# One-hot rows by a float32 compare on VectorE, a fourth buffer for table pieces, and another place for block 1's gates in a decoder layer

## The chip, the cores and the metric

The kernel runs on one core of one Trainium2 chip. TensorE (PE) multiplies, VectorE (DVE) and ScalarE (ACT) do element-wise work, GpSimd (POOL) asks for indirect gathers, SyncE (SP) asks for the plain transfers; 16 DMA engines move the data. Each engine works through its own list of instructions in order and waits at semaphores for the others. The metric is the device time of one execution in microseconds, less is better. The trace is of one profiled execution.

## What is computed

One decoder layer on 256 tokens of width 1024. Two attention parts come first; the change lies in the last part, product-key retrieval of single-neuron experts. Each of 8 heads picks 16 experts for a token, so that a token has 128; an expert's number is 128 x first index + second index:

```python
def peer(x, w_query, sub_keys_1, sub_keys_2, expert_down, expert_up):
    ...
    experts = jnp.take_along_axis(cand_idx, pos, axis=-1)
    gates = jax.nn.softmax(top_s, axis=-1)
    def block(args):
        xt, et, gt = args
        u = expert_down[et]
        act = jax.nn.gelu(jnp.einsum('td,tkd->tk', xt, u).astype(jnp.float32), approximate=False)
        vv = expert_up[et]
        return jnp.einsum('tk,tkd->td', (gt * act).astype(xt.dtype), vv)
```

Both tables have 16384 rows of 1024 float32 numbers, 64 MB each.

## The kernel before

The 256 tokens are two blocks of 128. After the attention parts, the top 16 experts of each head are picked on DVE (`pick`). From there the two blocks go different ways.

**Block 0 gathers.** `down` asks on GpSimd for one row of `expert_down` per token and pick, 128 gathers of 128 rows (a gather is called a *row* here: `gd`, 512 KB, five buffers), and DVE multiplies each with the block's hidden state and sums it into a column of `wt` (L899). Every 16 columns pass the gelu and are multiplied with their gates.

**Block 1 is dense.** `dense` reads the whole `expert_down` table, transposed, in 128 *pieces* of 128 experts (`d`, 512 KB each, three buffers, asked for by SyncE at L913) and multiplies each with the block's hidden state: 8 float32 matmuls of 128x128 a piece into PSUM (`sc`). Four pieces make a group; ScalarE takes the gelu of it into `W1` (expert's second index on partitions, then first index, then token).

**Spreading the gates.** `weights(b)` turns a block's 128 gates per token into the same layout. For each token one matmul is made (`wb`) of two one-hot matrices: `oa` on DVE (L1010; first index compared with 0 to 127, times the gate; four buffers) and `o2`, the second index compared with 0 to 127. `o2` is made for 8 tokens at a time: DVE compares in bf16 with the token innermost (`eq`, L990, against the table `iot8`), and ScalarE copies it to float32 with the token outermost (L1006). ScalarE brings four tokens' results from PSUM into `W0` (L1014). `weights(1)` spreads block 1's gates; `gates()` then multiplies them into `W1` for the first 27 groups (DVE, L1021), or copies them there for the last 5 groups (ScalarE, L1023), whose gelu is multiplied on later (L926). `weights(0)` then spreads block 0's finished weights into the same `W0`, and its transpose `tr` needs all 128 columns of `wt`.

**The up products.** For each of 128 pieces of `expert_up` (`u`), ScalarE and DVE split it in two float32r parts (`uh` L1153, `ul` L1154) and PE multiplies both blocks' weights with it. For 384 of the 1024 columns of block 0, up rows are gathered instead (`gu`, L931) and summed on DVE.

**Order.** A loop over `now` = 0 to 127 takes one row per step and, paced by `pace`, some dense pieces (`DPACE`) and some tokens of `weights(1)` (`SCAT1`). At step 78 the earlier buffers are closed. After the loop come the rest of `weights(1)`, all of `gates()`, and then a loop over 128 tokens of block 0 with the remaining pieces. A scheduler then sets the order on each engine from these priorities; only the up products keep the written order.

## Time and profile before

| | |
|---|---|
| time, median of 3 runs | 1080.87 us (1079.47 to 1081.7) |
| profiled execution | 1090.83 us |
| its span | 1089.0 us |
| mean granted clock of TensorE | 0.955 |
| PE busy | 947.3 us, 87% |
| DVE busy | 812.1 us, 75% |
| ACT busy | 479.2 us, 44% |
| POOL busy | 377.1 us, 35% |

Busy time is that of instructions that compute; idle time of an engine is put down to what ended it. Times in rows are us from the start of the span. The records of a float32 128x128 matmul come in pairs, so that a piece has 16 records and a token 2.

### The profile page before, as it was taken

How to read it: one execution, taken by the hardware profiler on the slowest of the kernel's cores; microseconds unless marked ns; L12 is line 12 of the kernel's file. 1: busy time of each engine (PE TensorE's matmuls, PEld its weight loads, DVE VectorE, ACT ScalarE, POOL GpSimd, SP SyncE). 2: the span in 40 equal slices, each digit the busy share in tenths (PEclk: the TensorE clock that was granted, in tenths of full speed). 3: DMA queues.
4: the chain of work that ended last, by engine and by line, in shares of the span. 5: the costliest groups of instructions: out<-in, count | busy, mean ns of one | idle time of the engine just before them, and what ended most of it. 6: DMA issues, size and time to landing. Idle time of an engine off the chain costs nothing.

```text
span 1089.0 us, 17849 instructions
## 1 busy us (share of the span) xinstructions
PE 947.3 (87%) x6650; PEld 881.0 (81%) x6650; DVE 812.1 (75%) x1944; ACT 479.2 (44%) x712; POOL 377.1 (35%) x263
## 2 busy tenths in 40 slices
PE   7999999897647957877788899899899999999994
PEld 6999879887547957766688799898788888888883
DVE  6957867556876987885478743765588888888887
ACT  5547664452101232221234344366655555555551
POOL 0000000001445452223345400000277777777773
PEclk9999999898888988999899999999899999999998
DMA  8454325444989789898899987744399999999992
GB/s 300 157 193 162 111 80 191 157 179 145 331 287 359 262 322 337 326 325 315 326 357 397 384 314 226 217 155 135 109 331 321 321 310 327 318 324 316 322 320 101
DMA packets 73974, 285.13 MB, mean 262 GB/s; under 512 B 9488, under 2 KB 10016, under 8 KB 67872
## 3 DMA queue, kind: packets, MB, share of 16 engines
q1 hardware_dynamic: 46976, 190.66, 50.2%
q0 software_dynamic: 26624, 92.29, 23.4%
q8 instruction: 52, 0.85, 0.3%
q10 hardware_dynamic: 288, 1.05, 0.3%
q14 instruction: 34, 0.28, 0.1%
HBM read 282.91 MB, written 1.05 MB: 261 GB/s over the span
## 4 chain that ended last, share of the span: by engine, by line
PE 68%; DMA 19%; DVE 6%; ACT 4%; issue 2%; POOL 0%; SPq 0%; ACTq 0%; DVEq 0%; POOLq 0%
PE py L74 27%; PE mm L74 18%; DMA d<-dnT 16%; PE sc L74 14%; PE wb L74 4%; DMA gd<-dn,ei 2%; PE tp L78 1%; DMA w<-xo 1%; DVE gd L899 1%; PE go L74 1%; ACT whi L235 1%; DVE wlo L237 1%; PE ks L74 1%; PE xo L74 1%; ACT o L1006 1%
## 5 line engine op out<-in xcount | busy, mean ns | idle before, releaser
L74 PE MATMUL sc<-h2T,d 128*128 128x128 f32 x2048 | 263.2, 287 | 61.6 <-DMA d<-dnT 58.8
L897 POOL DMA_INDIRECT gd<-dn,ei x128 | 151.7, 1185 | 469.4 <-ACT s1b L875 267.4
L74 PEld LDWEIGHTS sc<-h2T,d 128*128 128x128 f32 x2048 | 250.7, 201 | 69.8 <-DMA d<-dnT 42.9
L931 POOL DMA_INDIRECT gu<-upg,ei x128 | 220.7, 1724 | 224.3 <-DMA d<-dnT 144.0
L74 PE MATMUL py<-uh,w 128*128 128x320 f32 (+1 forms) x1024 | 234.5, 350 | 1.0 <-ACT uh L1153 1.0
L74 PEld LDWEIGHTS py<-uh,w 128*128 128x128 f32 x1024 | 176.4, 188 | 22.6 <-ACT uh L1153 1.2
L1153 ACT ACTIVATE uh<-u 128x1024 fp32r<-128x1024 f32 x128 | 135.8, 1062 | 117.5 <-PE py L74 117.5
L1154 DVE TENSOR_TENSOR ul<-u,uh 128x1024 fp32r<-128x1024 f32 x128 | 156.4, 1223 | 31.1 <-ACT uh L1153 31.1
L899 DVE CUSTOM_DVE_ANT_0 gd<-gd,h 128x1024 f32<-128x1024 f32 x128 | 154.4, 1218 | 20.8 <-DMA gd<-dn,ei 20.6
L74 PE MATMUL py<-ul,w 128*128 128x320 f32 (+1 forms) x512 | 138.3, 350 | 0.7 <-DVE ul L1154 0.7
L237 DVE TENSOR_TENSOR wlo<-w,whi 128x1024 fp32r<-128x1024 f32 (+1 forms) x68 | 81.3, 1197 | 47.4 <-PE mm L74 35.7
L1010 DVE TENSOR_SCALAR oa<-ii,ixT,wT 128x128 f32<-128x128 f32 x256 | 72.0, 347 | 56.7 <-PE wb L74 55.6
L74 PEld LDWEIGHTS py<-ul,w 128*128 128x128 f32 x512 | 90.7, 188 | 12.5 <-DVE ul L1154 1.0
L235 ACT ACTIVATE whi<-w 128x1024 fp32r<-128x1024 f32 (+1 forms) x68 | 70.4, 1039 | 54.2 <-PE mm L74 40.3
L74 PE MATMUL wb<-oa,o 128*128 128x128 f32 x512 | 73.1, 288 | 8.5 <-ACT o L1006 7.3
L1122 DVE SCALAR_TENSOR_TENSOR yq<-gu,wt,yq 128x384 f32<-128x384 f32 x127 | 77.9, 614 | 0.2
L74 PEld LDWEIGHTS wb<-oa,o 128*128 128x128 f32 x512 | 67.1, 201 | 9.8 <-ACT o L1006 7.9
L1014 ACT ACTIVATE W<-wb 128x512 f32<-128x512 f32 x64 | 37.9, 599 | 83.8 <-PE wb L74 83.2
L922 ACT ACTIVATE W<-sc 128x512 f32<-128x512 f32 x27 | 16.1, 598 | 116.9 <-PE sc L74 116.9
L1006 ACT ACTIVATE o<-eq 128x1024 f32<-128x1024 bf16 x32 | 65.8, 2072 | 1.8 <-DVE eq L990 1.8
L74 PE MATMUL mm<-whi,xPh 128*128 128x256 f32 (+1 forms) x176 | 50.8, 291 | 6.7 <-ACT xPh L244 6.7
L74 PE MATMUL mm<-h2T,w 128*128 128x128 f32 x448 | 54.0, 281 | 2.8 <-DMA w<-pq 2.8
(329 smaller groups left out, 1438.6 us busy)
## 6 DMA issues: line engine op xcount, KB each, us to landing
d<-dnT SPq DMA_DIRECT2D x128, 512.0 KB, 5.4
u<-upd SPq DMA_DIRECT2D x128, 512.0 KB, 4.7
w<-pq SPq DMA_DIRECT2D x10, 1024.0 KB, 5.8
w<-xo SPq DMA_DIRECT2D x8, 1024.0 KB, 4.8
w<-xk SPq DMA_DIRECT2D x4, 1024.0 KB, 5.4
w<-xv SPq DMA_DIRECT2D x4, 1024.0 KB, 4.8
w<-wo SPq DMA_DIRECT2D x4, 1024.0 KB, 4.8
w<-xq SPq DMA_DIRECT2D x4, 1024.0 KB, 4.8
```

The source lines that it names most:

```text
L74: self.eng.matmul(out, lhsT=lhsT, rhs=rhs, **kw)
L235: act.activation(hi, src, AF.Copy)
L237: eng.tensor_sub(lo, src, hi.bitcast(FT))
L897: gp.indirect_dma_start(out=g, out_offset=None, in_=I["dn"], in_offset=bass.IndirectOffsetOnAxis(ap=ei[:, k:k + 1], axis=0))
L899: vec.tensor_tensor_reduce(out=g, in0=g, in1=H2[0], scale=1.0, scalar=0.0, op0=OP.mult, op1=OP.add, accum_out=wt[:, k:k + 1])
L931: gp.indirect_dma_start(out=g, out_offset=None, in_=I["upg"], in_offset=bass.IndirectOffsetOnAxis(ap=PK[b]["ei"][:, k:k + 1], axis=0))
L1006: act.activation(o2, equal(b, 4 * g).rearrange("p k t -> p t k"), AF.Copy)
L1010: vec.tensor_scalar(a, iot, ixT[:, t:t + 1], wT[:, t:t + 1], op0=OP.is_equal, op1=OP.mult)
L1014: act.activation(W[0][:, :, 4 * g - 4:4 * g], ps[g - 1].rearrange("p (j i) -> p i j", j=4), AF.Copy)
L1122: vec.scalar_tensor_tensor(y, g, wt[:, k:k + 1], y, op0=OP.mult, op1=OP.add)
L1153: act.activation(uh, u, AF.Copy)
L1154: vec.tensor_sub(ul, u, uh.bitcast(FT))
```

## The change

The one-hot of the second index is written by DVE at once, as float32 and with the token outermost; the bf16 index, the table `iot8` and ScalarE's copy go. The pieces `d` get four buffers instead of three, and in the last loop every second piece uses one of the gathers' five. `SCAT1` ends at step 104 and not 116; 20 groups and not 27 come ahead of the gates, at nearly the same pace, up to step 103; the gates are taken at steps 104 to 110 of the gather loop and not behind it; from step 109 one piece is taken a step. The late groups' gelu shares the buffers of `o2`, and the gathered up rows have buffers of their own.

```diff
-SCAT1 = (80, 116)
-DENSE = 27
-DPACE = (46, 122)
+SCAT1 = (80, 104)
+DENSE = 20
+DPACE = 46
+DLATE = 1
 AHEAD = 2
+UH = 4
...
-        PK[b]["ix2"] = keep.tile([128, 128], BF, tag="ix2", name="ix2")
+        PK[b]["ix2"] = keep.tile([128, 128], FT, tag="ix2", name="ix2")
...
-                d = ust.tile([128, 8, 128], FT, tag="uh", name="d", bufs=3)
+                pool, tag, bufs = (gath, "gd", 5) if now == 127 and m % 2 else (ust, "uh", UH)
+                d = pool.tile([128, 8, 128], FT, tag=tag, name="d", bufs=bufs)
...
-                a = sml.tile([128, 4, 128], FT, tag="eq", name="ge", bufs=4)
+                a = ul_pool.tile([128, 4, 128], FT, tag="ul", name="ge", bufs=3)
...
-        g = sml.tile([128, 2 * CG], FT, tag="eq", name="gu", bufs=4)
+        g = sml2.tile([128, 2 * CG], FT, tag="gu", name="gu", bufs=4)
...
-        wT = sml2.tile([128, 128], FT, tag="wT", name="wT", bufs=2)
+        wT = sml2.tile([128, 128], FT, tag="wT", name="wT", bufs=1)
...
-                    act.activation(o2, equal(b, 4 * g).rearrange("p k t -> p t k"), AF.Copy)
+                    vec.tensor_tensor(o2, iot[:, None, :].to_broadcast([128, 8, 128]),
+                                      ix2[:, 4 * g:4 * g + 8, None].to_broadcast([128, 8, 128]), op=OP.is_equal)
...
         if 1 in W:
-            pace("dn", gd, 4 * DENSE, DPACE)
+            pace("dn", gd, 4 * DENSE, (DPACE, SCAT1[1] - 1))
         if 0 in W:
             pace("w1", gw[1], 133, SCAT1)
-    drain(gw[1], gates())
+        if now >= SCAT1[1]:
+            pace("gates", gg, 32, (SCAT1[1], SCAT1[1] + 6))
+        if now >= SCAT1[1] + 5 and now % DLATE == 0:
+            take(gd, 1)
+            at["dn"] += 1
     rest_d = 128 - 4 * DENSE
...
-        uh = ust.tile([128, DM], FR, tag="uh", name="uh", bufs=3)
+        uh = ust.tile([128, DM], FR, tag="uh", name="uh", bufs=UH)
```

What the scheduler makes of it, at three places. In these rows `ISA gd,wt` is the product of a gathered row with the hidden state and `ISA wt` its sum; `o` is `o2`. Line numbers of the change are two higher up to L990.

DVE, in the middle of the gathers, before: one stretch between two compares.

```order
L990 TENSOR_TENSOR eq<-iot_3906,ix_4802 128x1024
L1010 TENSOR_SCALAR oa<-ii,ixT,wT 128x128 x3
L899 ISA gd,wt<-gd,h_2923 128x1024
L899 ISA wt 128x1
L899 ISA gd,wt<-gd,h_2923 128x1024
L899 ISA wt 128x1
L1010 TENSOR_SCALAR oa<-ii,ixT,wT 128x128 x4
```

The same place in the change:

```order
L1008 TENSOR_SCALAR oa<-ii,ixT,wT 128x128 x5
L901 ISA gd,wt<-gd,h_2921 128x1024
L901 ISA wt 128x1
L901 ISA gd,wt<-gd,h_2921 128x1024
L901 ISA wt 128x1
L1008 TENSOR_SCALAR oa<-ii,ixT,wT 128x128 x6
L1003 TENSOR_TENSOR o_5444<-ii,ix_4787 128x1024
```

Between two pairs of rows there now stand five or six tokens, where three or four stood.

DVE, behind the last gathered row, before (the last `ISA wt` stands right ahead of it):

```order
L1010 TENSOR_SCALAR oa<-ii,ixT,wT 128x128 x8
L990 TENSOR_TENSOR eq<-iot_3906,ix_4802 128x1024
L1010 TENSOR_SCALAR oa<-ii,ixT,wT 128x128 x7
L990 TENSOR_TENSOR eq<-iot_3906,ix_4089 128x1024
L1010 TENSOR_SCALAR oa<-ii,ixT,wT 128x128 x8
L990 TENSOR_TENSOR eq<-iot_3906,ix_4089 128x1024
L1010 TENSOR_SCALAR oa<-ii,ixT,wT 128x128 x7
L990 TENSOR_TENSOR eq<-iot_3906,ix_4089 128x1024
L1010 TENSOR_SCALAR oa<-ii,ixT,wT 128x128 x11
L990 TENSOR_TENSOR eq<-iot_3906,ix_4089 128x1024
L1010 TENSOR_SCALAR oa<-ii,ixT,wT 128x128 x9
L1021 TENSOR_TENSOR W_3905<-W_3905,W_4835 128x512 x26
```

The end of the gathers in the change:

```order
L901 ISA gd,wt<-gd,h_2921 128x1024
L901 ISA wt 128x1
L1019 TENSOR_TENSOR W_3903<-W_3903,W_4821 128x512 x20
L929 TENSOR_TENSOR W_3903<-W_3903,ge 128x512 x2
L901 ISA gd,wt<-gd,h_2921 128x1024
L901 ISA wt 128x1
L901 ISA gd,wt<-gd,h_2921 128x1024
L901 ISA wt 128x1
L901 ISA gd,wt<-gd,h_2921 128x1024
L901 ISA wt 128x1
L906 TENSOR_TENSOR wt<-wt,gt 128x16
L929 TENSOR_TENSOR W_3903<-W_3903,ge 128x512
```

Block 1's 50 tokens that stood behind the last row are gone from there, and 20 gate multiplies and two late groups stand ahead of the last three rows.

PE, around the transpose of block 0's weights (`tr`), before:

```order
L74 MATMUL sc<-h2T,d 128x128 x16
L74 MATMUL wb<-oa,o_5969 128x128 x2
L74 MATMUL sc<-h2T,d 128x128 x72
L78 MATMUL tr<-ii,wt 128x128
L74 MATMUL wb<-oa,o_6211 128x128 x5
L74 MATMUL sc<-h2T,d 128x128
L74 MATMUL wb<-oa,o_6211 128x128 x2
L74 MATMUL sc<-h2T,d 128x128 x7
L74 MATMUL wb<-oa,o_6211 128x128
L74 MATMUL wb<-oa,o_6253 128x128 x5
L74 MATMUL sc<-h2T,d 128x128 x8
```

The same place in the change:

```order
L76 MATMUL sc<-h2T,d 128x128 x4
L76 MATMUL wb<-oa,o_5721 128x128 x2
L76 MATMUL sc<-h2T,d 128x128 x148
L80 MATMUL tr<-ii,wt 128x128
L76 MATMUL sc<-h2T,d 128x128 x4
L76 MATMUL wb<-oa,o_6088 128x128 x5
L76 MATMUL sc<-h2T,d 128x128
L76 MATMUL wb<-oa,o_6088 128x128 x3
L76 MATMUL wb<-oa,o_6117 128x128 x6
L76 MATMUL sc<-h2T,d 128x128
L76 MATMUL wb<-oa,o_6117 128x128 x2
L76 MATMUL wb<-oa,o_6147 128x128 x8
```

Counted over the whole list, the first token stands after 50 pieces before and 51 in the change, block 1's last token after 99 and 80.5, `tr` after 108 and 99; the rest of the 128 stand among block 0's tokens.

## Rows read from the trace of the kernel before

**Rows 1.** The chain that ended last, shares of the span by line, from the page.

```profile
PE py L74 27%; PE mm L74 18%; DMA d<-dnT 16%; PE sc L74 14%; PE wb L74 4%; DMA gd<-dn,ei 2%; PE tp L78 1%; DMA w<-xo 1%; DVE gd L899 1%; PE go L74 1%; ACT whi L235 1%; DVE wlo L237 1%; PE ks L74 1%; PE xo L74 1%; ACT o L1006 1%
```

**Rows 2.** Busy us by stretch: PE, PEld, DVE, ACT, POOL; PEclk, DMA share, GB/s.

```profile
400.00:520.00 120.00, 88.80 (x694) 84.66 (x693) 85.79 (x353) 27.90 (x58) 34.38 (x33) 0.94 0.90 329
...
544.00:632.00 88.00, 72.90 (x594) 70.44 (x593) 70.78 (x164) 32.73 (x36) 40.06 (x32) 0.96 0.99 381
632.00:683.00 51.00, 50.72 (x451) 50.53 (x452) 17.73 (x58) 22.74 (x27) 0.00 (x0) 1.00 0.77 253
...
703.00:783.00 80.00, 71.49 (x575) 70.41 (x576) 46.15 (x146) 48.26 (x53) 2.84 (x3) 0.94 0.38 126
783.00:1073.00 290.00, 289.30 (x1536) 256.03 (x1537) 256.71 (x319) 167.19 (x190) 217.87 (x125) 1.00 0.92 312
```

**Rows 3.** Tile `sc` alone: PE, PEld, DVE, ACT; PEclk, DMA share, GB/s.

```profile
544.00:632.00 88.00, 57.56 (x446) 53.50 (x445) 0.00 (x0) 4.17 (x7) 0.96 0.99 381
632.00:683.00 51.00, 41.11 (x343) 39.67 (x344) 0.00 (x0) 2.98 (x5) 1.00 0.77 253
```

**Rows 4.** The same for tile `oa`: PE, PEld and DVE busy, clock, DMA.

```profile
544.00:632.00 88.00, 21.14 (x148) 19.68 (x148) 22.32 (x78) 0.96 0.99 381
632.00:683.00 51.00, 14.51 (x108) 13.27 (x108) 14.06 (x50) 1.00 0.77 253
```

**Rows 5.** The chain in order of time: start, us, what; two pieces, seven tokens.

```profile
664.30 3.57 PE sc L74 x32
...
738.50 1.66 PE wb L74 x14
```

**Rows 6.** Waits from 520 to 544 us: total, times, longest.

```profile
DVE eq L990 <- ACT ix L753: 10.2, 1, 10.2
```

**Rows 7.** Waits from 544 to 632 us.

```profile
DVE oa L1010 <- PE wb L74: 11.1, 11, 3.0
...
POOL gd L897 <- DVE oa L1010: 3.6, 6, 2.1
...
DVE gd L899 <- DMA gd<-dn,ei: 1.2, 2, 1.0
```

**Rows 8.** Waits from 632 to 683 us.

```profile
DVE oa L1010 <- PE wb L74: 19.1, 9, 3.4
```

**Rows 9.** Waits from 703 to 783 us.

```profile
PEld wb L74 <- ACT o L1006: 7.9, 3, 3.1
```

**Rows 10.** DVE in order of time: start, us, line, what, count, idle before.

```profile
512.70 1.22 DVE L899 CUSTOM_DVE_ANT_0 gd<-gd,h 128x1024 f32<-128x1024 f32 x1
...
513.85 1.22 DVE L899 CUSTOM_DVE_ANT_0 gd<-gd,h 128x1024 f32<-128x1024 f32 x1
...
544.62 1.11 DVE L1010 TENSOR_SCALAR oa<-ii,ixT,wT 128x128 f32<-128x128 f32 x4
...
683.06 15.74 DVE L1021 TENSOR_TENSOR W<-W,W 128x512 f32<-128x512 f32 x26 [4.72 <-ACT W L1014]
...
701.90 0.35 DVE L1010 TENSOR_SCALAR oa<-ii,ixT,wT 128x128 f32<-128x128 f32 x1
...
702.76 2.81 DVE L1010 TENSOR_SCALAR oa<-ii,ixT,wT 128x128 f32<-128x128 f32 x10
```

**Rows 11.** PE in order of time: the last pieces and the first up product.

```profile
779.84 1.95 PE L74 MATMUL sc<-h2T,d 128*128 128x128 f32 x16
782.82 0.56 PE L74 MATMUL py<-uh,w 128*128 128x320 f32 x2 [1.03 <-ACT uh L1153]
```

**Rows 12.** Groups of instructions (busy us, mean ns of one), and a DMA issue (us to landing).

```profile
L1154 DVE TENSOR_TENSOR ul<-u,uh 128x1024 fp32r<-128x1024 f32 x128 | 156.4, 1223 | 31.1 <-ACT uh L1153 31.1
...
L1006 ACT ACTIVATE o<-eq 128x1024 f32<-128x1024 bf16 x32 | 65.8, 2072 | 1.8 <-DVE eq L990 1.8
...
L990 DVE TENSOR_TENSOR eq<-iot,ix 128x1024 bf16<-128x1024 bf16 x32 | 21.7, 689 | 24.0 <-ACT o L1006 13.6 <-ACT ix L753 10.2
...
d<-dnT SPq DMA_DIRECT2D x128, 512.0 KB, 5.4
```

More of the change, by code (lines that the diff above doesn't have):

```diff
@@ L849 @@
     for b in B2:
-        PK[b] = dict(ei=keep.tile([128, 128], I32, tag="ei", name="ei"),
-                     gt=keep.tile([128, 128], FT, tag="gt", name="gt"),
-                     wt=keep.tile([128, 128], FT, tag="wt", name="wt"),
+        PK[b] = dict(gt=keep.tile([128, 128], FT, tag="gt", name="gt"),
                      sel=work.tile([128, 2, 128], FT, tag="qi", name="sel", bufs=2))
+    PK[0]["ei"] = keep.tile([128, 128], I32, name="ei", bufs=1)
+    PK[0]["wt"] = keep.tile([128, 128], FT, name="wt", bufs=1)
     S12 = {}
@@ L985 @@
     W = {}
-    def equal(b, t0):
-        eq = sml.tile([128, 128, 8], BF, tag="eq", name="eq", bufs=4)
-        vec.tensor_tensor(eq, iot8, PK[b]["ix2"][:, None, t0:t0 + 8].to_broadcast([128, 128, 8]), op=OP.is_equal)
-        return eq
     def weights(b):
-        ixT = PK[b]["ixT"]
-        wT = sml2.tile([128, 128], FT, tag="wT", name="wT", bufs=2)
+        ixT, ix2 = PK[b]["ixT"], PK[b]["ix2"]
+        wT = sml2.tile([128, 128], FT, tag="wT", name="wT", bufs=1)
         pt = smt("tr")
@@ L1039 @@
     gw = [weights(b) for b in B2]
-    gd = dense()
-    ust = sml = iot8 = None
+    gd, gg = dense(), gates()
+    ust = sml = None
     def make_room():
-        nonlocal sml, ust, iot8
+        nonlocal sml, ust
         ctxL.close()
@@ L1049, in make_room @@
         W[1] = big.tile([128, 128, 128], FT, name="W1")
-        iot8 = sml.tile([128, 128, 8], BF, tag="eq", name="iot8", bufs=4)
-        act.copy(iot8, iot[:, :, None].to_broadcast([128, 128, 8]))
     gpick = {}
@@ L1092 @@
             py = [[pyy.tile([128, 512], FT, name="py%d%d" % (b, i)) for i in B2] for b in B2]
-            dg = sml2.tile([128, 128], FT, tag="dg", name="dg", bufs=1)
+            dg = sml2.tile([128, 128], FT, tag="oa", name="dg", bufs=OA)
             act.activation(dg, ident, AF.Copy, scale=ALPHA)
```

## The prediction

> **What bounds the kernel now.** I began with the shares of the chain that ended last [rows 1]: the up products take 27%, the projections 18%, and between them the dense products `sc` with their table pieces (`d<-dnT`) and the gate spreading `wb` some 34%. The change touches only that middle part, so I cut it into stretches by the engines' rows [rows 2]. From 400 to 520 us PE is busy 88.80 of 120 us with DMA at a 0.90 share; PE waits for pieces. From 544 to 632 us, rows being gathered and block 1's tokens spread, DMA is at 0.99 and 381 GB/s: transfers are the limit, PE has 72.90 of 88 us, DVE 70.78. From 632 to 683 us PE is full (50.72 of 51) and DVE nearly idle (17.73): here the backlog of pieces and tokens is worked off that did not fit beside the gathers. Then come 20 us in which DVE applies the gates, and from 703 to 783 us block 0's tokens are spread while the last 20 pieces run (128 - 108); PE is busy 71.49 of 80, DMA at 0.38. From 783 to 1073 us PE is busy 289.30 of 290, whatever happened earlier. So the time is where PE starts its first up product, 782.82 us [rows 11], plus a tail that the change leaves alone.
>
> **Prices.** A piece (8 matmuls, two records each) takes PE 3.57 / 2 = 1.79 us, a token 1.66 / 7 = 0.24 us [rows 5]. On DVE a token's `oa` takes 2.81 / 10 = 0.28 us, a gathered row 513.85 - 512.70 = 1.15 us, a gate multiply 15.74 / 26 = 0.61 us [rows 10]. The new one-hot is a float32 compare of 1024 per partition with both inputs broadcast; the trace has none. Bounds: 0.69 us, the bf16 compare that it replaces, and 2.07 us, ScalarE's reordering copy [rows 12]. I take 1.22 us, `ul`, the DVE row with the same number of elements and the same width.
>
> **The change part by part.** *Compare.* ScalarE loses 32 copies x 2.07 = 66 us, DVE gains 32 x (1.22 - 0.69) = 17 us. ScalarE was on the path only where a matmul waited for that copy, 7.9 us from 703 to 783 [rows 9]; DVE is busy only 46.15 of the 80 us there [rows 2].
>
> *A fourth piece buffer, 400 to 544 us.* PE waited there for pieces, and DVE's first compare waited 10.2 us for the index copy behind PE's transpose [rows 6]. Block 1's first `oa` came at 544.62 us [rows 10]. More buffers help until transfers are the limit: the 329 x 120 = 39.5 MB of 400 to 520 us take 104 us at 381 GB/s [rows 2], so at most 16 us are won; nothing is won if DVE's own work sets the pace. The compare still waits for the same place on PE (dense piece 45), which now comes earlier. I take half, 8 us: first `oa` at 536.6.
>
> *Tokens of block 1, all beside the gathers.* In PE's order the first token stands after 51 pieces in the change, its last after 80.5 (99 before); in DVE's, the tokens stand between rows 91 and 123, where before only 78 were done when the last row was. Work from first to last token: PE 29.5 x 1.79 + 128 x 0.24 = 83.5 us. DMA 29.5 + 32 transfers of 0.524 MB = 32.2 MB, at 381 GB/s 85 us. DVE 32 x 1.15 + 128 x 0.28 + 13 x 1.22 = 88.5 us (three compares stand ahead). DVE becomes the narrowest, by little, and to it come its waits. From 544 to 632 us `oa` waited 11.1 us for PE in 78 tokens [rows 4, 7], 0.142 us each; 128 x 0.142 = 18 us. The other measured value is 19.1 us in 50 tokens, 0.38 each, where PE was full [rows 4, 8]: 49 us. I take the first, since the change has 0.23 pieces per token on PE against 0.36 there and 0.43 in the second (343 records [rows 3] to 50 tokens). So 107 us, last token at 643.3. Queued behind a waiting `oa` on DVE are rows, so a long wait would also stop the gathers.
>
> *Gates, 12 late groups, up to the second transpose.* PE has 99 - 80.5 = 18.5 pieces before it can transpose block 0's weights: 33 us, to 676.4. The 20 gate multiplies cost nothing beside that: DVE waits for the last spread (4.72 us before [rows 10]), multiplies 20 x 0.61 = 12.2 us, does two late groups (their pieces, up to the 88th, are through by then) and the last three rows, 3.5 us, together about 25 us. ScalarE's 12 copies instead of 5 lie in the same 33 us. Without that cover, that is, if DVE were over 8 us later, each us would be paid. Block 0's first `oa` follows the transpose by 0.6 us: 677.0 against 701.90 [rows 10].
>
> *Block 0's tokens with the rest of the pieces.* 29 pieces are left, not 20: PE 29 x 1.79 + 128 x 0.24 = 82.6 us. The first 48 tokens have one piece among them, so DVE leads: 24 x 0.28 + 3 x (1.22 + 8 x 0.28) = 17 us against 13 on PE, 4 more. 1 us to the first up product, as before (779.84 + 1.95 to 782.82 us [rows 11]). [...] The 7 more late multiplies, 4.3 us of DVE, hide under PE.
>
> *At nothing:* the index table's copy goes; four up rows are asked for on GpSimd's queue between gathers, waiting on the same dense piece as DVE's compare; SyncE no longer fetches five `u` pieces in between but after the last `d`, whose slot frees eight pieces (14 us) before PE ends; shared tags and one `wT` buffer (its two uses lie 100 us apart).
>
> **The sum.** 677.0 + 88 = 765.0 against 782.8: 17.8 us less. The profiled execution took 1090.83 us (span 1089.0, 1.83 around it), 10 us over the median of 1080.87; I take the difference over whole: 1080.87 - 17.8 = 1063 us.
>
> **The rivals.** *PE leads the tokens (slower).* The waits of DVE's `oa` are 0.38 us a token, as from 632 to 683 us, not 0.142; rows stand behind them, so DMA starves, pieces come late and the 8 us are not won either: 31 + 8 = 39 us more, 1102 us. It decides from 0.22 us a token (28 us of waits) without the 8 us; with them from 0.28. For it: four `oa` buffers, engines that run in order, and PE, DMA and DVE within 5 us of each other. Against: fewer pieces per token.
>
> *Everything closes up (faster).* Transfers run at 381 GB/s from 400 us on (16 us won, not 8), the waits halve (9, not 18), and DVE's lead at block 0's start is hidden (3): 20 us more, 1043 us. For it: DMA at 0.90 there, and no copy of ScalarE between compare and matmul. Against: DVE's own picks.
>
> *SyncE's queue holds the pieces.* Late pieces use the gather's buffers, and their loads wait in order for rows 124 to 128 to be read; piece 98 stands behind one that waits for row 126, which DVE reads after the gates, about 4.7 + 12.2 + 1.2 + 3.5 = 21.6 us after the last token. With 5.4 us to land [rows 12] it is there after 27 us, and PE wants it after 17.5 x 1.79 = 31. So there are 4 us to spare; a DVE later by 14 us costs 10: 1073 us.
>
> *GpSimd is kept from asking for rows.* From 544 to 632 us a gather waited 3.6 us in six pieces for `oa` [rows 7], for 78 of them; for 128 that makes 6 us, hidden behind five row buffers, since DVE waited only 1.2 us for rows there [rows 7]. If all 128 x 0.28 = 36 us were paid, the time would be 1099 us. [...]
>
> **How the numbers follow.** Forecast, 1052 to 1070 us: 0.50. Closes up, below 1052: 0.20. SyncE's queue, 1070 to 1078: 0.10. No change, when one of these eats all: 0.05. PE leads, 1084 to 1102: 0.12. GpSimd: 0.03. The range leaves out the best few hundredths and the two slow cases: 1041 to 1081. About 0.2% (2.2 us) is what a measurement of this kernel can tell from no change; so faster 0.80, same 0.05, slower 0.15.
>
> **What would show it.** In the profile after: block 1's first `oa` before 540 us and its last near 643, with DVE above 80% between; `oa` waiting for PE some 18 us there; PE without gaps from there to the transpose near 676; first up product near 765, and from there 290 us as before. Wrong if the first token does not come earlier (the buffer), if `oa` waits over 28 us (PE leads), if the compare takes 2 us rather than 1.22 (13 more us of DVE in the stretch), or if PE waits for `d` after 645 us (SyncE's queue).

## The result, and the profile after

The changed kernel takes 1048.43 us, median of 4 runs (1042.45 to 1050.36), against 1081.28 for the kernel before measured beside it (4 runs, 1079.47 to 1082.02): 33 us less, a ratio of 0.969 with a 95% interval of 0.966 to 0.973. The forecast was 1063 us, with 1041 to 1081 as its range. So the sign was right and the time lies in the range, but the gain is 15 us larger than forecast, and the time falls below 1052 us, where the rival "everything closes up" had put it.

The profiled execution of after took 1042.45 us (span 1040.7), 6 us under its median; that of before was 10 us above its own. The two spans therefore differ by 48 us, of which part is scatter. One piece of that scatter can be seen: the first dense matmul comes at 386.6 us here and at 397.1 in before, though PE's instructions ahead of it are the same in both; up to 386 us the granted clock was 0.96 here and 0.94 in before. I therefore measure stretches from the first dense matmul on.

The chain of after, by line, answers [rows 1]:

```profile
PE py L76 28%; PE mm L76 17%; PE sc L76 10%; DMA d<-dnT 9%; DMA gd<-dn,ei 4%; DVE gd L901 4%; DVE oa L1008 3%; PE wb L76 3%; DVE o L1003 2%; POOL gd L899 1%; PE tp L80 1%; DVE wlo L239 1%; DMA w<-xo 1%; PE go L76 1%; ACT whi L237 1%
```

The wait for table pieces (`d<-dnT`) fell from 16 to 9%, `sc` from 14 to 10%, and VectorE has come onto the chain: rows (`gd`), tokens (`oa`) and the new compare (`o`), 9% together.

Busy time by stretch (PE, PEld, DVE, ACT, POOL, then granted clock, DMA share, GB/s); the first two rows answer those of [rows 2], the third is the token stretch of after:

```profile
400.00:520.00 120.00, 98.06 (x769) 90.56 (x769) 95.59 (x358) 26.06 (x57) 49.18 (x41) 0.96 1.01 392
544.00:632.00 88.00, 83.80 (x703) 82.42 (x702) 78.01 (x174) 24.86 (x45) 34.34 (x25) 0.96 0.95 363
...
515.80:603.00 87.20, 85.35 (x722) 83.98 (x722) 85.73 (x208) 23.40 (x41) 46.63 (x33) 0.97 0.95 362
```

From 400 to 520 us transfers now run at 392 GB/s, not 329, and PE is busy 98 us, not 89. In the token stretch DVE is busy 85.7 of 87.2 us, without the waits that I had added to it; PE is busy 85.4 of them, so both are full there.

VectorE in order of time (start, us, line, what, count, idle before it): block 1's first tokens, the last before the gates, the gates, block 0's first tokens; then PE's first up product. They answer [rows 10, 11]:

```profile
515.79 3.29 DVE L1008 TENSOR_SCALAR oa<-ii,ixT,wT 128x128 f32<-128x128 f32 x9
...
602.77 0.61 DVE L1008 TENSOR_SCALAR oa<-ii,ixT,wT 128x128 f32<-128x128 f32 x2
...
607.26 12.13 DVE L1019 TENSOR_TENSOR W<-W,W 128x512 f32<-128x512 f32 x20
...
645.69 1.63 DVE L1008 TENSOR_SCALAR oa<-ii,ixT,wT 128x128 f32<-128x128 f32 x6
```

```profile
732.89 0.56 PE L76 MATMUL py<-uh,w 128*128 128x320 f32 x2 [1.03 <-ACT uh L1153]
```

From these rows, and the same rows of every kernel that I ran, comes the table on which the rest stands (us; "tokens" is from block 1's first `oa` to its 128th, "behind" from there to the transpose of block 0's weights, "block 0" from its first `oa` to the first up product; 1 to 2 us between the last two are left out). From the first to the last up product every kernel takes 290.1 to 291.7 us, so that part is untouched, as forecast.

| kernel | time, median | first dense matmul at | to block 1's first oa | tokens | behind | block 0 | first dense matmul to first up product |
|---|---|---|---|---|---|---|---|
| before | 1081.3 | 397.1 | 147.5 | 133.4 | 23.3 | 80.9 | 385.7 |
| before_again | 1085.9 (one run) | 392.3 | 149.3 | 130.3 | 23.7 | 80.0 | 384.0 |
| after | 1048.4 | 386.6 | 129.2 | 87.2 | 42.0 | 87.2 | 346.3 |
| three_bufs | 1078.2 | 390.4 | 148.5 | 92.1 | 45.9 | 87.2 | 374.3 |
| old_pace | 1052.7 | 393.6 | 130.1 | 125.8 | 20.3 | 71.9 | 349.8 |
| three_old | 1075.0 | 387.8 | 150.2 | 133.6 | 23.2 | 70.3 | 378.6 |
| pace_only | 1090.5 | 396.2 | 148.8 | 97.2 | 40.8 | 99.5 | 387.6 |
| own_slots | 1047.5 | 393.8 | 131.0 | 87.7 | 41.1 | 87.2 | 347.7 |
| gates_spread | 1049.2 | 398.8 | 129.6 | 87.9 | 41.8 | 87.2 | 347.1 |
| dense24 | 1060.6 | 393.3 | 150.8 | 106.6 | 34.9 | 64.8 | 357.7 |
| mid110_22 | 1045.9 | 386.3 | 129.7 | 108.1 | 26.5 | 80.9 | 347.4 |
| compare_twice | 1079.8 | 391.7 | 129.0 | 86.0 | 60.2 | 102.5 | 380.1 |
| five_four | 1055.1 | 405.1 | 123.7 | 90.6 | 38.0 | 87.2 | 340.2 |
| five_ul2 | 1040.5 | 394.4 | 124.5 | 86.3 | 40.2 | 88.2 | 339.9 |

### The profile page after: what moved, and what is told of

Read it like the earlier page. It is cut to its first block, busy times and chain, and to the rows that moved or that the text cites. A ratio compares the mean times of both kernels' runs of the same rounds, so it can differ in the third digit from the quotient of the medians.

```text
span 1040.7 us, 17837 instructions
## 1 busy us (share of the span) xinstructions
PE 937.0 (90%) x6650; PEld 870.2 (84%) x6650; DVE 826.9 (79%) x1944; ACT 420.2 (40%) x686; POOL 386.9 (37%) x263
## 4 chain that ended last, share of the span: by engine, by line
PE 62%; DVE 14%; DMA 14%; issue 4%; ACT 3%; POOL 1%; SPq 0%; ACTq 0%; POOLq 0%; DVEq 0%
PE py L76 28%; PE mm L76 17%; PE sc L76 10%; DMA d<-dnT 9%; DMA gd<-dn,ei 4%; DVE gd L901 4%; DVE oa L1008 3%; PE wb L76 3%; DVE o L1003 2%; POOL gd L899 1%; PE tp L80 1%; DVE wlo L239 1%; DMA w<-xo 1%; PE go L76 1%; ACT whi L237 1%
## 5 line engine op out<-in xcount | busy, mean ns | idle before, releaser
L899 POOL DMA_INDIRECT gd<-dn,ei x128 | 160.6, 1255 | 430.9 <-ACT s1b L877 268.3
L76 PE MATMUL sc<-h2T,d 128*128 128x128 f32 x2048 | 255.0, 280 | 25.9 <-DMA d<-dnT 24.6
L76 PEld LDWEIGHTS sc<-h2T,d 128*128 128x128 f32 x2048 | 242.6, 195 | 32.9 <-DMA d<-dnT 16.2
L901 DVE CUSTOM_DVE_ANT_0 gd<-gd,h 128x1024 f32<-128x1024 f32 x128 | 155.2, 1224 | 23.8 <-DMA gd<-dn,ei 23.7
L76 PEld LDWEIGHTS py<-ul,w 128*128 128x128 f32 x512 | 91.1, 189 | 12.5 <-DVE ul L1154 1.0
L1008 DVE TENSOR_SCALAR oa<-ii,ixT,wT 128x128 f32<-128x128 f32 x256 | 72.5, 359 | 23.3 <-PE wb L76 22.5
L76 PEld LDWEIGHTS mm<-h2T,w 128*128 128x128 f32 x448 | 53.7, 200 | 4.1 <-DMA w<-pq 4.1
L76 PE MATMUL mm<-wlo,xPh 128*128 128x256 f32 (+1 forms) x176 | 52.0, 296 | 1.6 <-DVE wlo L239 1.6
```

Source lines behind the costliest of these rows:

```text
L76: self.eng.matmul(out, lhsT=lhsT, rhs=rhs, **kw)
L899: gp.indirect_dma_start(out=g, out_offset=None, in_=I["dn"], in_offset=bass.IndirectOffsetOnAxis(ap=ei[:, k:k + 1], axis=0))
L901: vec.tensor_tensor_reduce(out=g, in0=g, in1=H2[0], scale=1.0, scalar=0.0, op0=OP.mult, op1=OP.add, accum_out=wt[:, k:k + 1])
L1008: vec.tensor_scalar(a, iot, ixT[:, t:t + 1], wT[:, t:t + 1], op0=OP.is_equal, op1=OP.mult)
```

## The experiments

My theory after the result was this: the fourth piece buffer is most of the gain, VectorE's own work limits the tokens, and pieces held in SyncE's queue cost 9 us behind them. The rivals: the compare or the pacing brought the gain; transfers or TensorE limit the tokens; late gelus delay the pieces.

**The kernel before once more.**

> The kernel before, unchanged, a second look. Two questions. The first dense matmul came at 397.1 us of the span in the first profile of before and at 386.6 us in that of after, although nothing ahead of it was changed. If that is scatter between executions, this look shows another value than 397, anywhere from 386 to 397, and the time from the first dense matmul to block 1's first oa stays at 147 us, from there to the first up product at 238 us. If it is a property of the kernel before, the first dense matmul comes at 397 again (within 2 us).

The first dense matmul came at 392.3 us, and over all kernels here at 386 to 399 us (405 where row buffers were taken away). So that place differs by some 12 us between kernels whose PE instructions ahead of it are the same, and by 5 us between two executions of before. Behind it the two traces of before agree within 2 us in the sum.

**The fourth buffer taken away.**

```
-UH = 4
+UH = 3
```

> The kernel after with three buffers for the table pieces in place of four; compare, pacing and gates as after. My theory: the fourth buffer is what brings block 1's first oa nearer to the first dense matmul (147.5 us in before, 129.2 in after), so this goes back by 10 to 18 us to 139 to 147, PE waits for d in that stretch 20 us and more rather than 13, and the time is 8 to 18 us over after's: 1056 to 1066. Rival, the compare or the pacing brought it: 129 to 132 us, time within 3 us of after's 1048. Rival, pieces are missed later, beside the tokens, as well: over 18 us more, 1067 and up.

The time is 1078.24 us (10 runs; 0.994 of before, 0.989 to 0.998): 30 us of the 33 are gone. That is more than the theory's 8 to 18, and the third case. The stretch up to the first `oa` went back to 148.5 us (147.5 in before), 19.3 us more than in after; another 4.9 went beside the tokens and 3.9 behind them. Here are the same stretches, from the first dense matmul to the first `oa`, of before, after, this kernel, and a five-buffer kernel further down (its later part), in that order:

```profile
397.00:544.00 147.00, 110.25 (x817) 103.92 (x818) 100.02 (x380) 35.24 (x65) 47.06 (x43) 0.92 0.90 330
```

```profile
387.00:515.00 128.00, 105.36 (x831) 97.48 (x830) 101.07 (x384) 29.45 (x63) 54.84 (x45) 0.97 1.01 394
```

```profile
391.00:539.00 148.00, 113.98 (x830) 106.56 (x829) 101.08 (x382) 28.92 (x62) 49.76 (x45) 0.92 0.91 335
```

```profile
400.00:515.00 115.00, 100.45 (x803) 92.60 (x801) 93.42 (x365) 27.92 (x61) 44.40 (x39) 0.99 1.02 401
```

Three buffers give a DMA share of 0.90 to 0.91 and 330 to 335 GB/s, with either compare; four give 1.01 and 394. PE's waits for pieces there (total, times, longest), before and after:

```profile
PE sc L74 <- DMA d<-dnT: 41.3, 22, 7.5
```

```profile
PE sc L76 <- DMA d<-dnT: 20.2, 19, 5.8
```

Why three are too few could have been read in the trace of before. This is its row of issues from 400 to 520 us (count, KB, median us from issue to landing):

```profile
d<-dnT SPq DMA_DIRECT2D x44, 512.0 KB, 6.2
```

A buffer is taken for 6.2 us of transfer and 1.8 us of matmuls, so three buffers pass a piece every 8.0 / 3 = 2.67 us at best, an estimate; measured were 147.5 us for 50.6 pieces, 2.9 each. Four would allow 2.0 by the same estimate; measured were 129.2 / 51.1 = 2.53, with DMA at a share of 1.01, so there the transfers are near their limit.

**The old pacing, with compare and four buffers.**

```
-SCAT1 = (80, 104)
-DENSE = 20
-DPACE = 46
-DLATE = 1
+SCAT1 = (80, 116)
+DENSE = 27
+DPACE = (46, 122)
...
-            pace("dn", gd, 4 * DENSE, (DPACE, SCAT1[1] - 1))
+            pace("dn", gd, 4 * DENSE, DPACE)
...
-        if now >= SCAT1[1]:
-            pace("gates", gg, 32, (SCAT1[1], SCAT1[1] + 6))
-        if now >= SCAT1[1] + 5 and now % DLATE == 0:
-            take(gd, 1)
-            at["dn"] += 1
+    drain(gw[1], gg)
```

> The compare, the fourth buffer and the shared tags of after, but the pacing of before: block 1's tokens up to row 116, 108 pieces among the rows, all gates applied after the last row. From the first dense matmul to the first up product before took 385 us, after 346; three buffers under after's pacing took 374. My theory: the fourth buffer keeps its 19 us up to the first oa, and the pacing is worth the rest, so 362 to 368 us from first dense matmul to first up product, and a time of 1064 to 1071. Rival, the pacing brings nothing by itself (tokens gained there are lost before the second transpose): 346 to 352 us, 1048 to 1054. Rival, the buffer only pays with the new pacing: 375 to 385, 1075 and up.

1052.73 us (0.970 of before, 0.964 to 0.976), and 349.8 us from the first dense matmul to the first up product: the rival. All of the moved work is worth 4 us by the medians, 2 to 4 by the traces. The table shows where it goes: the tokens take 125.8 us instead of 87.2, 38.6 more, but 20.3 instead of 42.0 behind them and 71.9 instead of 87.2 in block 0, 37.0 less. Most of what the new pacing saves beside the rows is PE's own work put later: 97 pieces lie ahead of block 1's last token with the old pacing, 80.5 with the new, and 16.5 pieces x 1.79 = 30 us.

**The pacing alone, on the kernel before** (three buffers, the bf16 compare and ScalarE's copy).

```
-SCAT1 = (80, 116)
-DENSE = 27
-DPACE = (46, 122)
+SCAT1 = (80, 104)
+DENSE = 20
+DPACE = 46
+DLATE = 1
...
-            pace("dn", gd, 4 * DENSE, DPACE)
+            pace("dn", gd, 4 * DENSE, (DPACE, SCAT1[1] - 1))
...
-    drain(gw[1], gates())
+        if now >= SCAT1[1]:
+            pace("gates", gg, 32, (SCAT1[1], SCAT1[1] + 6))
+        if now >= SCAT1[1] + 5 and now % DLATE == 0:
+            take(gd, 1)
+            at["dn"] += 1
```

> The kernel before (bf16 compare, ScalarE's copy, three piece buffers) with the pacing of after: tokens up to row 104, gates among the last rows, late groups behind them. After with three buffers stood at 1078. My theory: pacing alone brings little while pieces come late; to the 1078 come ScalarE's copies, 8 us of waits in block 0's tokens and as much at most in block 1's, so 1076 to 1088, not measurably better than before. Rival, the pacing is worth what my prediction gave it, about 10 us on its own: 1066 to 1073. Rival, VectorE has 17 us less to do with the bf16 compare and is the limit beside the rows: 1060 to 1066.

1090.47 us (10 runs; 1.004 of before, 1.0004 to 1.008): by itself the pacing makes the kernel no faster, rather a little slower. That is above the 1076 to 1088 of my theory, and both rivals fall. Waits in block 0's tokens, 684 to 784 us:

```profile
DVE oa L1011 <- PE wb L75: 37.9, 26, 2.3
...
PEld wb L75 <- ACT o L1007: 10.8, 5, 2.9
PE wb L75 <- ACT o L1007: 9.9, 5, 2.7
```

PE waits some 10 us for ScalarE's copy. With the new compare (three_bufs, the same pacing and buffers) those rows are gone and the stretch takes 87.2 us, not 99.5; the whole takes 374.3, not 387.6.

**The compare alone,** old_pace with three buffers; the edit on top of the old pacing is

```
-UH = 4
+UH = 3
```

> The compare of after alone: three piece buffers and the pacing of before. It fills the last corner: with the new compare and four buffers the old pacing took 349.8 us from the first dense matmul to the first up product, the new pacing 347; with three buffers the new pacing took 374. My theory: the compare takes ScalarE's copies out of block 0's tokens (80.5 us in before, 71.9 with the old pacing and four buffers) and shortens block 1's a little, so 366 to 372 us and a time of 1067 to 1075, and the fourth buffer is worth 17 to 22 us here against 27 with the new pacing. Rival, the compare brings something only with the new pacing: 380 to 385 us, 1078 to 1082, and the buffer is then worth 30 under either pacing.

1074.95 us (10 runs; 0.998 of before, 0.994 to 1.002). The traces give 378.6 us against 384.0 and 385.7, some 6 us less, all of it in block 0 (70.3 against 80 to 81); the timing can't tell that from no change. My theory had wanted 366 to 372 us, and the rival 380 to 385. The fourth buffer is worth 28.8 us of the traces with the old pacing (378.6 - 349.8) and 28.0 with the new. So buffer and pacing don't depend on each other, and the 17 to 22 us of my theory for the buffer were too few. The buffer with the bf16 compare was not tried.

**The late pieces in their own buffers.**

```
-                pool, tag, bufs = (gath, "gd", 5) if now == 127 and m % 2 else (ust, "uh", UH)
+                pool, tag, bufs = ust, "uh", UH
```

> The kernel after, but the late pieces of the table keep to their own four buffers; none uses a buffer of the gathered rows. My theory: between block 1's last oa and the second transpose (42.0 us in after for 18.5 pieces, 33 predicted) pieces come late because their loads stand in SyncE's queue behind loads that wait for rows 124 to 128 to be read on VectorE. Then this stretch takes 33 to 36 us and the time falls by 6 to 9 us, to 1039 to 1043. Rival, the pieces are late for the late groups' gelu and multiplication (DVE waited 12.8 us for ScalarE's ge there): the stretch stays at 41 to 43 us, time 1047 to 1050. Rival, without the rows' buffers four buffers are too few there: longer than 43 us, over 1050.

1047.52 us (0.964 of before, 0.956 to 0.972), 41.1 us behind the tokens: nothing changed. The waits of SyncE's queue around there, after first (596 to 646 us), then this kernel (604 to 650):

```profile
SPq L916 <- PE sc L76: 29.4, 18, 3.9
SPq L916 <- DVE wt L901: 4.1, 1, 4.1
```

```profile
SPq L916 <- PE sc L76: 26.9, 17, 3.8
...
SPq L1152 <- DVE wt L901: 3.5, 1, 3.5
```

The load of a late piece that waits for a row (`wt`) is there in after and gone here, but a load of `u` (L1152) now stands in its place in the queue and waits nearly as long, 3.5 us. So the edit did not clear the queue, and the unchanged time alone does not refute my theory. The traces bound it. The piece for which PE then waits is asked for right behind that load: at 605.70 us in after, at 614.89 here, and at 618.98 in gates_spread (below). By the turn of the four buffers, PE had done with the piece that held its buffer at 604.65, 614.17 and 617.93 us. So the queue kept that load back by at most 0.7 to 1.1 us, of a wait of 3.1 us. The rest is the time to landing: 7.4 to 7.7 us in the three, while PE had three pieces left, 5.4 us.

**The gates spread between the last rows.**

```
-        for g in range(32):
+        for g in (*range(DENSE, 32), *range(DENSE)):
...
-            pace("gates", gg, 32, (SCAT1[1], SCAT1[1] + 6))
+            pace("gates", gg, 32, (SCAT1[1], SCAT1[1] + 22))
```

> The kernel after with the 12 copies of the late groups' gates first and the 20 multiplications spread between rows 104 and 126, where after has them in one run of 12 us. In after, five rows were read close together just ahead of that run (602 to 606 us), their five buffers were asked for again at once, TensorE waited 3.1 us for a piece at 610 us while transfers stood at 1.03 of their share, and its granted clock was then 0.5 to 0.6 for 6 us. My theory: that bunch is most of the 9 us that I missed between block 1's last oa and the second transpose (42 us for 18.5 pieces); spread out, it takes 33 to 37 us, time 1041 to 1045. Rival, the pieces are late there whatever the gates do, since the last rows still share the transfers: 40 to 43 us, 1046 to 1050. Rival, multiplications wait for the spreading copies and hold up rows that stand behind them: over 44 us, 1051 and up.

1049.20 us, 41.8 us behind the tokens: the rival, the run of gates isn't it. PE right behind block 1's last token, in after, own_slots and gates_spread:

```profile
603.76 6.42 PE L76 MATMUL sc<-h2T,d 128*128 128x128 f32 x56
613.26 15.59 PE L76 MATMUL sc<-h2T,d 128*128 128x128 f32 x112 [3.08 <-DMA d<-dnT]
```

```profile
613.28 6.42 PE L76 MATMUL sc<-h2T,d 128*128 128x128 f32 x56
622.75 1.57 PE L76 MATMUL sc<-h2T,d 128*128 128x128 f32 x6 [3.05 <-DMA d<-dnT]
```

```profile
617.03 6.42 PE L76 MATMUL sc<-h2T,d 128*128 128x128 f32 x56
626.54 1.83 PE L76 MATMUL sc<-h2T,d 128*128 128x128 f32 x7 [3.09 <-DMA d<-dnT]
```

The same wait, 3.05 to 3.09 us, at the same piece, 3.5 pieces behind the last token, in all three. What happens around it in after, by stretch:

```profile
604.00:610.00 6.00, 6.00 (x56) 5.99 (x54) 5.12 (x9) 5.97 (x12) 0.06 (x1) 1.00 1.03 412
610.00:614.00 4.00, 0.92 (x5) 0.77 (x4) 4.00 (x8) 1.42 (x3) 0.00 (x0) 0.80 1.03 410
614.00:620.00 6.00, 6.00 (x34) 6.00 (x33) 5.99 (x10) 0.00 (x0) 0.00 (x0) 0.56 0.48 172
```

Transfers stand at 410 GB/s while the last rows are fetched. With no more tokens between the pieces PE uses up what it has at 1.79 us a piece and then waits; after the wait the granted clock is 0.56 for 6 us, 34 records where 6 us at a granted clock of 1.00 held 56. The wait and these 22 records (22 x 0.11 us) make 5.5 of the 9 us, three later waits of 0.4 to 0.5 us for pieces 1.3; the rest is spread. Late gelus hold nothing up there; from 603 to 646 us PE waits for pieces alone, and the gelu (`ge`) waits for PE:

```profile
PE sc L76 <- DMA d<-dnT: 4.4, 4, 3.1
ACT ge L928 <- PE sc L76: 21.5, 3, 12.1
```

Nor does a fifth piece buffer remove the wait. In the last kernel below (five_ul2) PE gets through 5.5 pieces and then waits as long:

```profile
605.95 10.04 PE L76 MATMUL sc<-h2T,d 128*128 128x128 f32 x88
619.16 26.42 PE L76 MATMUL sc<-h2T,d 128*128 128x128 f32 x208 [3.17 <-DMA d<-dnT]
```

That the transfers, shared with the last rows, make the pieces land so late is argued from these rows; no kernel tested it by itself.

**More pieces ahead.**

```
-DENSE = 20
+DENSE = 24
```

> The kernel after with 96 pieces of the table among rows 46 to 104 in place of 80 (the gates multiply 24 groups, 8 are late). Block 1's first token then stands behind 60 pieces, not 51. From the first dense matmul to the first up product after has 346 us, of which TensorE needs 128 x 1.79 + 256 x 0.24 = 290. My theory: ahead of the first oa TensorE waits for pieces because rows take the transfers; with more pieces per row it waits less in sum, and the time falls by 3 to 8 us, to 1040 to 1045. Rival, transfers are the limit there and each of the 9 pieces more delays rows and tokens by 1.3 us, which VectorE then can't make up: first oa 12 us later, time 1050 to 1060.

1060.55 us (0.977 of before, 0.970 to 0.983): the rival, and more. The first `oa` comes 22 us later, not 12: 102 rows are read ahead of it, in after 91, so 11 more rows had shared the transfers with the 9 more pieces. Block 0 is 22 us shorter (it has fewer pieces left), and the tokens take 19 us more.

**A pace in between.**

```
-SCAT1 = (80, 104)
-DENSE = 20
+SCAT1 = (80, 110)
+DENSE = 22
```

> The kernel after with block 1's tokens paced to row 110 instead of 104 and 88 pieces ahead of the gates instead of 80 (the same pieces per row). With the tokens packed as in after, VectorE was busy 98% of that stretch and TensorE then waited for pieces while the last rows were fetched, 42 us for 18.5 pieces; with the old pacing (to row 116) TensorE lost 13 us beside the tokens and nothing behind them. My theory: in between, part of both is saved: 338 to 344 us from the first dense matmul to the first up product (after 347), time 1040 to 1046. Rival, what is saved behind the tokens is lost beside them, as with the old pacing: 347 to 351 us, 1048 to 1053.

1045.92 us (4 runs, 1041.60 to 1051.57), and 347.4 us from the first dense matmul to the first up product. The time lies at the upper end of my theory's 1040 to 1046, but the stretch, which my theory wanted at 338 to 344, is the rival's. It lies between the two pacings in each stretch, and the sum is the same as in after.

**Each compare issued twice.**

```
                     vec.tensor_tensor(o2, iot[:, None, :].to_broadcast([128, 8, 128]),
                                       ix2[:, 4 * g:4 * g + 8, None].to_broadcast([128, 8, 128]), op=OP.is_equal)
+                    vec.tensor_tensor(o2, iot[:, None, :].to_broadcast([128, 8, 128]),
+                                      ix2[:, 4 * g:4 * g + 8, None].to_broadcast([128, 8, 128]), op=OP.is_equal)
```

> The kernel after with every float32 compare issued twice (the second writes the same values again), so 32 more VectorE instructions of about 1.2 us. My theory: VectorE's own work sets block 1's token stretch (87.2 us from the first oa to the 128th, work by the prediction 88.5 with 13 compares in it). Then that stretch takes 13 x 1.2 = 16 us more, about 103 us, three more compares ahead of it add up to 3.6 us, those of block 0 lie mostly under TensorE, and the time rises by 13 to 19 us to 1061 to 1068. Rival, TensorE or the transfers set the stretch (83.5 and 85 us by the prediction) and VectorE has room: stretch 87 to 92 us, time 1048 to 1053.

1079.81 us (10 runs; 0.997 of before), 31 us over after for 32 x 1.22 = 39 us of VectorE's work; but not as expected. The tokens take 86.0 us, as in after, which is nearest to the rival's 87 to 92. The scheduler had put the rows further back: at the 128th `oa` 107 rows are read, in after 123. So this is no clean test of the token stretch by its length. VectorE's sum there, 128 x 0.28 + 18 rows x 1.15 + 26 compares x 1.22 = 88 us, is again about the whole stretch:

```profile
520.70:606.70 86.00, 83.89 (x705) 82.66 (x706) 84.59 (x193) 22.59 (x40) 22.03 (x18) 0.97 0.82 281
```

DMA is at 0.82 there: transfers had room, so they do not set the 86 us. But PE had as little room as VectorE (83.9 and 84.6 us busy). The chain that ended last takes PE for 64 of the 86 us here; it takes VectorE for 71 of 87 in after, and PE for 69 of 88 in own_slots, whose tokens are those of after. So VectorE and PE are both full, and which of them sets the stretch is not shown; no kernel here eased one of them alone. The delayed rows then came due behind the tokens (60.2 us), where PE waited 11.0 us for one piece and SyncE's queue five times for rows (12.5 us in all):

```profile
662.33 3.35 PE L76 MATMUL sc<-h2T,d 128*128 128x128 f32 x14 [10.96 <-DMA d<-dnT]
```

```profile
SPq L916 <- DVE wt L901: 12.5, 5, 3.8
```

That is the picture that the rival "SyncE's queue" had drawn; it needs a VectorE that is later than in after.

**Five buffers for pieces, four for rows.**

```
-    gath = ctx.enter_context(tc.tile_pool(name="gath", bufs=5))
+    gath = ctx.enter_context(tc.tile_pool(name="gath", bufs=4))
...
-UH = 4
+UH = 5
```

> The kernel after with five buffers for the pieces and four for the rows (before and everywhere else five). With the fourth piece buffer transfers ran at 394 GB/s from the first dense matmul to the first oa, three gave 330 to 335. My theory: with four the transfers are the limit, so a fifth brings nothing there (first oa 127 to 131 us after the first dense matmul), and in the 3.1 us wait behind the last token it can bring at most those 3 and the slow clock behind them: time 1042 to 1050; four row buffers cost up to 5 us elsewhere, since weight halves of earlier parts use them too. Rival, pieces still come late for want of buffers: first oa at 118 to 124 us, time 1036 to 1042. Rival, rows are late with four buffers, VectorE waits for them: over 1055.

1055.09 us (0.979 of before, 0.973 to 0.985), the time of the last rival. VectorE did wait longer for rows, 30.5 us from the first dense matmul to the transpose against 14.6 in after, but that part is no longer for it: the first `oa` is 5 to 6 us nearer to the first dense matmul (123.7) and the first up product 6 to 7 (340.2), but the first dense matmul itself comes at 405.1 us, later than in any other trace: the parts ahead keep weight halves in the row buffers. So the first `oa` is the first rival's (118 to 124), and the loss lies ahead: a fifth buffer still gives something.

**Five and five,** the room taken from `ul`.

```
-UH = 4
+UH = 5
...
-                a = ul_pool.tile([128, 4, 128], FT, tag="ul", name="ge", bufs=3)
+                a = ul_pool.tile([128, 4, 128], FT, tag="ul", name="ge", bufs=2)
...
-                    o2 = ul_pool.tile([128, 8, 128], FT, tag="ul", name="o2", bufs=3)
+                    o2 = ul_pool.tile([128, 8, 128], FT, tag="ul", name="o2", bufs=2)
...
-            ul_pool = ctxB.enter_context(tc.tile_pool(name="ulp", bufs=3))
+            ul_pool = ctxB.enter_context(tc.tile_pool(name="ulp", bufs=2))
...
-        ul = ul_pool.tile([128, DM], FR, tag="ul", name="ul", bufs=3)
+        ul = ul_pool.tile([128, DM], FR, tag="ul", name="ul", bufs=2)
```

> The kernel after with five piece buffers beside five row buffers; the room comes from ul, two buffers in place of three (one-hots, late gelus and the up stage's low parts share them). With five and four the stretch from the first dense matmul to the first oa fell from 130 to 123.7 us and the one to the first up product from 347 to 340, while the parts ahead of it, which use the row buffers for weights, lost some 11 us. My theory: with both at five the 7 us stay and nothing is lost ahead: first dense matmul at 386 to 399 us of the span, then 338 to 343 to the first up product, 290 to 292 from there to the last: 1038 to 1044. Rival, two ul buffers make TensorE wait for VectorE in the up stage or for one-hots: more than 294 us from the first to the last up product, or over 347 before it, and 1048 or more.

1040.54 us (6 runs, 1036.89 to 1042.26; 0.960 of before, 0.957 to 0.963): as my theory had it, and faster than both kernels, 8 us under after. 339.9 us lie between first dense matmul and first up product, 290.1 in the up stage with two `ul` buffers. The issues of pieces from 394 to 519 us suggest that a sixth would bring little; it was not tried:

```profile
d<-dnT SPq DMA_DIRECT2D x50, 512.0 KB, 8.8
```

A piece now lands 8.8 us after its issue, where it took 6.2 in before, and the rate went only from 394 GB/s in after to 401; that it waits behind other transfers is read into these two figures, not shown.

## Why the prediction was right, and where it was short

**The sum.** In the profiled spans I had the first up product at 765.0 us; it came at 732.9, 32 us earlier. By my steps: the first `oa` at 515.8, not 536.6 (20.8 us, of which 10.5 lie ahead of the first dense matmul, where PE's instructions are the same); the tokens 87.2 us, not 107 (19.5); behind them 42.0, not 33 (-8.9); block 0 87.2, not 88 (0.8; the 88 is 82.6 + 4 + 1, rounded). As the profiled execution of after was a low one and that of before a high one, 15 of the 32 us remain between the medians.

That the time lies in the range is in part luck. I had put 8 us on the fourth buffer and 9.8 on all the rest. By the medians the buffer brought 30 (1078.2 to 1048.4) and the rest 3 (1081.3 to 1078.2): one was far too small and the other too large, and the range was 40 us wide.

**The fourth buffer: right in kind, sized at less than half.** I put 8 us on it, "at most 16". Measured from the first dense matmul it gave 19 to 20 us up to the first `oa`, with either pacing, and 28 in the whole. Two things were wrong. I bounded the bytes of the 120 us from 400 to 520, but pieces were late over 147 us, up to the first `oa`. And I halved the bound for fear of VectorE's own work, though VectorE had 100 of 147 us and PE waited 41 us for pieces in plain view. Had I set issue-to-landing plus matmuls against three buffers, as above, the want of buffers would have been plain. The 381 GB/s that I took for the limit of transfers was about right (394 here).

**The tokens beside the rows: the work right, the waits not.** I put 88.5 us of work on VectorE, and the stretch took 87.2, VectorE busy for 85.7 of them. That it alone is the limit, as I had it, is not shown: PE is busy 85.4 us, so that by these shares no more than 1.9 us was to be won there from VectorE alone, an estimate. The 18 us of waits did not come. VectorE's waits in after's stretch, from the list of all (516 to 603 us), are one:

```profile
DVE gd L901 <- DMA gd<-dn,ei: 0.8, 1, 0.8
```

I had taken 0.142 us a token from before's 544 to 632 us, 11.1 us of waits for PE, and never asked what PE was waiting for there. It waited for pieces:

```profile
PE sc L74 <- DMA d<-dnT: 13.8, 12, 2.9
```

The two go together in the other kernels as well. With three buffers PE waits 12.4 us for pieces and VectorE 14.4 us for PE under the old pacing (three_old, 538 to 626 us), 2.0 and 2.7 under the new (three_bufs, 539 to 631 us). With four buffers PE waits there for no piece, and VectorE for PE 1.4 us under the old pacing (old_pace, 524 to 612 us) and not at all under the new. So these were PE's waits for pieces, handed on; pacing and buffer both take them away, and the term should have been near nothing. The reverse wait is small too. In after's stretch PE waits for `oa` twice, and the longer of the two, 8.2 us, is the wait for the first token of all:

```profile
PE wb L76 <- DVE oa L1008: 9.1, 2, 8.2
```

The rival "PE leads" wanted 0.38 us of waits per token and did not come either, full as PE was.

**The price of the compare: right.** 1.22 us was taken from `ul`. The row of after (busy us, mean ns of one):

```profile
L1003 DVE TENSOR_TENSOR o<-ii,ix 128x1024 f32<-128x1024 f32 x32 | 39.1, 1228 | 5.4 <-PE sc L76 5.4
```

`ul` took 1223 ns for as many elements [rows 12]; this row, 1228 ns, shows that a compare with two broadcast inputs costs the same here. My bounds of 0.69 and 2.07 us were wider than needed. ScalarE's 7.9 us of waits in block 0 went as forecast: 80 to 70 us with the old pacing (three_old), 99.5 to 87.2 with the new.

**The moved work: right stretch by stretch, wrong in what it is worth.** I gave the moves and the compare 9.8 us together. By the traces compare and new pacing with three buffers gave 385 - 374 = 11, so that sum looks right; but the compare makes 6 (with the old pacing) to 13 of it (with the new), and the pacing 4 to -3. I had seen that PE would have 29 pieces left for block 0 instead of 20 and 18.5 ahead of the transpose, and the work in those stretches was right. I missed that this must nearly cancel: PE needs 128 x 1.79 + 256 x 0.24 = 290 us from its first dense matmul to its first up product in any order. What counts is how much of the time it isn't at work, or is at work at a lower granted clock (0.92 in before and 0.97 in after up to the first `oa`): 385 - 290 = 95 us in before, 56 in after, 50 with five buffers, 60 with the old pacing.

**Behind the tokens: 9 us too little.** I counted 33 us of PE work and no gap. The gap came where the rows' last transfers and the pieces met, with the granted clock at 0.56 from 614 to 620 us behind it. The rival "SyncE's queue" named this place and what happens there: the awaited piece does stand behind a load that waits for a row. But that makes at most 1.1 of the 3.1 us (own_slots); the rest is the time to landing, whose cause is argued only.

**GpSimd: off the path as forecast, but the waits misread.** In after, 516 to 603 us:

```profile
POOL gd L899 <- DVE wt L901: 23.7, 11, 3.4
POOL gd L899 <- DVE oa L1008: 15.4, 16, 5.9
```

I had read such waits (3.6 us in before's stretch) as a price of each `oa`. They are waits for a row buffer. Ten of the 16 are 0.3 us, as between any two gathers here, and so are five of the six in before. Each of the other six ends within 0.6 us of VectorE having read a row, with the first or second `oa` behind it: the longest, 5.9 us up to 524.28, follows the row that was read from 522.78 to 524.00. The 11 waits for `wt` end with the row itself. So these waits show no gather held up by an `oa` itself, and no run here shows whether an `oa` ever stops one. VectorE waited 0.8 us for rows in the stretch, so the end was not reached.

## What to carry to other kernels

Set the time from a load's issue to its landing, plus the time of its use, against the number of its buffers, before any reordering: one more buffer gave 28 us here, the reordering next to nothing. When work is moved, add up what the bounding engine still has to do to the end of the whole part and count only the time in which it does nothing; a stretch that gets shorter has often handed its work to the next. Before a wait goes into a forecast, look at what the engine that was waited for was itself waiting for: if the change removes that, the wait goes too.

## What was not expected of the hardware

The transfers of one core ran at 392 to 412 GB/s over stretches of 4 to 128 us, where the stretch of before that I took for the limit had shown 381. A wait of PE of 3.1 us cost some 2.4 us more in after, since the granted clock was at 0.56 from 614 to 620 us behind it; behind the same wait it was at 0.72 in own_slots (622 to 628 us) and in gates_spread (626 to 632 us). And executions differ much ahead of the first dense matmul alone: it came at 386.3 to 398.8 us among kernels whose PE instructions are the same up to there, at 392.3 and 397.1 for the kernel before itself. A comparison of two profiled spans needs a mark that both share.
